# Marking the selected keys on VectorE behind the last pair's mask, a later sum of the gate rows, and an earlier load of the second modulation tile

## The chip, the core and the metric

One core of a Trainium2 chip runs the whole step in one launch. The engines are TensorE (PE in the profile; its weight loads are PEld), VectorE (DVE), ScalarE (ACT), GpSimd (POOL) and SyncE (SP), which issues most transfers. The metric is the device time in microseconds; the runs are compared by their median.

## The reference, cut to what matters

One layer of a decoder: sparse attention with an indexer and retention, side by side, for 1024 new prompt rows and 8 sequences of 4 sample rows (1056 rows in all, D = 1024), all in float32.

```
mod = silu(c) @ w_ada + b_ada;  shift, scale, gate = split(mod, 3)
h   = rms_norm(x, g_norm) * (1 + scale) + shift
qa, ka, va, za, qi, ki, wi, qr, kr, vr, zr, ga, gr = split(h @ w_in)
# sparse attention: score every key with the indexer, keep 256
scores = sum_h relu(qi_h . ki) * wi_h
idx    = top_k(where(admissible, scores, -inf), 256)      # ties: lower index first
y_a    = softmax(qa . ka[idx] / 8) @ va[idx] * silu(za)
# retention: 8 heads, chunks of 128, decay by head; rotary on qr, kr
out    = (q k^T * dmat) v + (q state) * q_decay;  state = decay * state + (k * k_decay)^T v
y_r    = group_norm(out) * g_ret * silu(zr)
merged = sigmoid(ga) * (y_a @ w_pa) + sigmoid(gr) * (y_r @ w_pr)
y      = rms_norm(x + gate * (merged @ w_out), g_final)
```

The keys, values, indexer keys and retention states are outputs too.

## The kernel before, in words

**Products.** PE multiplies float32 matrices as three products of two-part numbers: the high part of the weights with the high part of h, the high part with the low part, and the low part with the high part (L218 to L220, in `terms`). A projection of 128 columns of w_in is 3 chunks of 352 rows, each 8 tiles of the depth times 3 products, so 72 products of 128x352. Each weight tile (512 KB, `ws`) is loaded on SP's queue, rounded by ScalarE (`wh`, L204) and its rest is taken by VectorE or, every third time, by GpSimd (`wl`, L205).

**The head (0 to 62 us).** x is transposed and squared; for each of the 8 depth tiles, `load_wa(k)` loads two tiles of w_ada, `modulation(k)` multiplies them with silu(c) (`ada_rows`, L212) and turns the result, and `h_tile(k)` scales and shifts the tile of h (L340), rounds it (`HH`, ScalarE, L348) and takes the rest (`HL`, VectorE, L349). The first two weight tiles of w_in are loaded behind the first w_ada tile; they are rounded on ScalarE and their rests taken on VectorE (L400). `start_two` (L235) runs the first two projections tile by tile, as the tiles of h arrive.

**The indexer (62 to 140 us)** gives the scores SC[2..7] of the prompt's row blocks (blocks 2 to 7, 384 to 1024 columns wide) and SCS of the sample rows (1056 wide).

**Retention (140 to 545 us)** is four pairs of heads, p = 0 to 3. A pair projects KR, QR, VR, ZR and QA. VR and KR are turned to token rows (PE L543, evicted by ScalarE into `vtok`, L584, and `kd`, L587); z is evicted as `zt` and `zsT` (L595, L596). Then the decayed states (`S`, L611), the products within chunks (PE L621), which VectorE multiplies with the decay mask (L627; the last of the four in a pair is kept as `masked[p]`), and the outputs. The sample rows' small products follow (L663; VectorE's masks `ss`, L666; PE L671). Then the group norm: sums and squares, an rsqrt in 18 columns on VectorE (L162 to L175), the scaling on GpSimd (L695), the transposes back (PE L703), and the last multiplication (`normed[p]`, L706). Behind each pair come a gate's projection, the gate rows (`gate_rows`: products with a part of w_ada, L212 again, a copy by ScalarE L523, a sum over four row groups by PE L525, a second copy L526 and a small transfer L527), and a second gate's projection.

**The selection beside it.** `pick_all` finds for each row of a block the 256th largest score by 31 steps over the bits of the number: VectorE counts for blocks 2 to 6 (L870), ScalarE for block 7 and SCS. The steps stand between the projections of pairs 0 to 3, placed behind entries of `marks`, which hold VectorE's and ScalarE's last instruction at the end of each projection chunk. `exact` repairs thresholds near zero; then `finish(j)` marks the keys of a block: a count above the threshold (L870), the number of ties still to be taken (L918), the row of ties (`eq`, GpSimd, L922), its running sum (L923), two compares (L924, L925), and the multiplication by -1e30 into the mask `bi` (ScalarE, L926). In code order SCS comes first; behind `normed[2]` block 7, then blocks 2 and 3; behind `masked[3]` and one mark each, blocks 4, 5, 6. All blocks share one `eq` and one `ra` tile. The masks of the sample rows are read from 540 us on, those of the blocks in the prompt's attention, from about 820 us.

The rest is the sample attention with its gathers and the projections of K, V and Z (545 to 820 us), the prompt's attention (820 to 960) and the merge.

The order of each engine's instructions is fixed when the kernel is built: a scheduler takes the instructions by their priority in the code and by the `issue_after` marks, and each engine then runs its list in order. What waits holds up everything behind it on that engine.

Of the kernel before, what the change touches and what calls it, by code (L numbers as in the profile page):

```python
# [9 lines left out]
F32R = mybir.dt.float32r  # L10
BF = mybir.dt.bfloat16
I32 = mybir.dt.int32
# [105 lines left out]
def _hybrid_step(ctx, tc, A, outs, dbg):  # L118
# [122 lines left out]
    with ExitStack() as s0:  # L241
# [92 lines left out]
        def h_tile(k, pm):  # L334

            shift = BB[:, k, 0:1]
            nc.scalar.activation(AA[:, k], pm[:, 9:18], AF.Identity, bias=cg[:, k:k + 1], scale=cols[:, 24 + k:25 + k])
            nc.scalar.activation(shift, pm[:, 0:1], AF.Identity, bias=cols[:, k:k + 1])
            h = XT[:, k]
            nc.vector.scalar_tensor_tensor(h[:, :T], h[:, :T], AA[:, k, 0:1], RB[:, :T], op0=OP.mult, op1=OP.mult)  # L340

            nc.vector.tensor_scalar(BB[:, k, 1:9], pm[:, 1:9], cols[:, k:k + 1], shift, op0=OP.add, op1=OP.subtract)
            hs = h[:, T:].rearrange("p (b i) -> p b i", b=NB)
            by_seq = lambda ab: ab[:, k, 1:9].unsqueeze(2).to_broadcast([128, NB, NI])
            nc.vector.tensor_tensor(hs, hs, by_seq(AA), op=OP.mult)
            nc.vector.tensor_tensor(hs, hs, by_seq(BB), op=OP.add)
            for sl in (slice(0, 528), slice(528, TT)):
                high = nc.scalar.activation(HH[k][:, sl], h[:, sl], AF.Identity, bias=shift)  # L348
                rest = nc.vector.scalar_tensor_tensor(HL[k][:, sl], h[:, sl], shift, f32(HH[k][:, sl]), op0=OP.add, op1=OP.subtract)  # L349
            return high, rest  # L350
# [19 lines left out]
        zeros = sp.tile([128, 640], BF, name="zeros")  # L370
        nc.vector.memset(zeros, 0.0)

        def idle_products(n, behind):

            x = pl()
            with tc.issue_after(behind):
                for i in range(n):
                    nc.tensor.matmul(x[:, 512 * (i % 2):512 * (i % 2) + 512], zeros[:, :128], zeros[:, 128:], start=True, stop=True)

        for k in range(KT):  # L380
            load_wa(k)
            if k == 0:
                with tc.issue_after(loads[-1].ins):
                    ws = [wload(wp, w_in, f, 128) for f in (O_KI, O_QI)]
                pm, turned = modulation(k)
                idle_products(8, turned)
            else:
                with tc.issue_after(spread):
                    pm, turned = modulation(k)
            head_ends = h_tile(k, pm)  # L390
            if k == 0:
                for i in (0, 1):
                    wh, wl = [sp.tile([128, KT, 128], F32R, name="w", bufs=4) for _ in "hl"]
                    if i == 0:
                        nc.scalar.copy(wh, ws[i])
                    else:
                        with tc.issue_after(head_ends[0].ins):
                            nc.scalar.copy(wh, ws[i])
                    with tc.issue_after(head_ends[1].ins):
                        nc.vector.tensor_sub(wl, ws[i], f32(wh))  # L400
                    W.append((wh, wl))
# [96 lines left out]
    def retention(gp):  # L498
        with ExitStack() as s3:
# [7 lines left out]
            for p in range(4):  # L507
                rows = split_rows(gp, O_QA + 128 * p, p, q_rows, qs)
                pair(rp, RC, O, SD, p, rows)
                for _ in rows:  # L510
                    pass
                gates(gp, (4 + 2 * p,))
                gate_rows(rp, p)
                gates(gp, (5 + 2 * p,))

    def gate_rows(rp, p):
# [7 lines left out]
        x = pj()  # L524
        nc.tensor.matmul(x[:32, :256], C[:, C_SEL:C_SEL + 32], parts_, start=True, stop=True)  # L525
        nc.scalar.copy(sums[:9], x[:9, :256])  # L526
        nc.scalar.dma_start(GD[:, 256 * p:256 * p + 256], sums[:9])  # L527
# [188 lines left out]

    k_out, v_out, ki_out, st_out, ks_out, vs_out, kis_out, sts_out = outs[2:]

    with ExitStack() as s1:
# [4 lines left out]
        with ExitStack() as s2:  # L724
# [74 lines left out]
            gidx = selp.tile([128, NB], I32, name="gidx")  # L799
            gio = ip.tile([128, NB], I32, name="gio")  # L800
            nc.sync.dma_start(gio, A["gio"])
            with tc.issue_after(whole_row):
                nc.vector.tensor_scalar(ptab, ptab, 16, None, op0=OP.mult)
                nc.vector.tensor_tensor(gidx, ptab, gio, op=OP.add)
            SX = ip.tile([128, 260], F32, name="sx")
# [108 lines left out]
        def finish(j):  # L914
# [7 lines left out]
            nc.gpsimd.tensor_scalar(eq[:n, :W], sc, t, 1.0, op0=OP.is_equal, op1=OP.mult)  # L922
# [3 lines left out]
            nc.scalar.activation(bi, ra[:n, :W], AF.Copy, scale=MASKNEG)  # L926
# [9 lines left out]
        def pick_all():  # L936
# [20 lines left out]
            with tc.issue_after(normed[2].ins):  # L957
                for j in (NP - 2, NV - 1, NV - 2):
                    finish(j)
            for i, j in enumerate(range(NV - 3, -1, -1)):  # L960
                with tc.issue_after(masked[3].ins), tc.issue_after(marks[73 + i][0]):
                    finish(j)
# [75 lines left out]
    QU = 2  # L1038
    NQ = 8 // QU
# [9 lines left out]
    idx = sv.tile([128, NQ, NB], I32, name="idx")  # L1049
    for u in range(NQ):  # L1050
        nc.vector.tensor_scalar(idx[:, u], gidx, float(NQ), float(u), op0=OP.mult, op1=OP.add)
# [452 lines left out]
```

## Time and profile before

| | us |
|---|---|
| median of 3 runs | 1117.72 |
| the runs | 1115.03 to 1120.34 |
| the profiled execution, its own time | 1117.12 |
| its span, first to last instruction | 1115.3 |
| PE busy in it | 1085.7 |
| VectorE busy | 680.3 |
| ScalarE busy | 478.0 |
| GpSimd busy | 253.4 |

The profile is one execution. Its mean granted PE clock was 0.993 of full speed. Rows of the timeline have the start and the length in us, the engine, the line, the operation, the tile written and those read, the shapes, and, in brackets, the idle time of the engine just before and what ended it. "x16" at the end of a PE row is a run of instructions joined to one row. Rows of the windows have, for each stretch, the busy time of each engine, the granted PE clock (1.00 is full), the share of the transfer engines and GB/s. The wait lines have the total, the number of times and the longest in us.

### The profile page before, as it was taken

The numbers are of one execution on the slowest core, as the hardware profiler recorded it, in microseconds if no ns is written. First come the engines' busy times: TensorE is split into PE (matmuls) and PEld (weight loads), VectorE is DVE, ScalarE is ACT, GpSimd is POOL, SyncE is SP. The second block draws the span as 40 slices with busy tenths as digits, with TensorE's granted clock in tenths as the row PEclk, the third lists the DMA queues.
The fourth block names the chain that finished last, engine by engine and source line by source line (L and its number), as shares of the span: only waits on it lengthen the run. The fifth ranks groups of instructions, "written<-read, shape, count | busy, mean of one in ns | idle before, by whom it ended". The sixth has DMA issues, their size and how long they took to land. (4 is left out here: it accounts for less than half of the span.)

```text
span 1115.3 us, 20512 instructions
## 1 busy us (share of the span) xinstructions
PE 1085.7 (97%) x8137; PEld 987.9 (89%) x8138; DVE 680.3 (61%) x1632; ACT 478.0 (43%) x923; POOL 253.4 (23%) x202
## 2 busy tenths in 40 slices
PE   7999999999999999989999999999999999999997
PEld 6889899899989989989999998887988888898776
DVE  6776349698877868888422222210356777497765
ACT  6574445554654455333343333311335666443211
POOL 0003006113311220263242222244113333100000
PEclk9999999999999999999999999999999999999999
DMA  9923335265244515523787757386797520367431
GB/s 308 243 72 105 112 101 151 54 203 140 82 149 126 164 46 181 155 61 92 256 286 232 234 183 247 112 286 240 243 310 273 182 99 30 111 202 257 152 122 58
DMA packets 156024, 185.63 MB, mean 166 GB/s; under 512 B 18630, under 2 KB 126990, under 8 KB 154839
## 3 DMA queue, kind: packets, MB, share of 16 engines
q1 hardware_dynamic: 145632, 147.80, 42.5%
q0 software_dynamic: 9856, 35.66, 9.5%
q8 instruction: 64, 1.05, 0.4%
q10 hardware_dynamic: 438, 0.86, 0.2%
q14 instruction: 34, 0.27, 0.1%
HBM read 139.33 MB, written 41.17 MB: 162 GB/s over the span
## 5 line engine op out<-in xcount | busy, mean ns | idle before, releaser
L218 PE MATMUL pj<-hh,wh 128*128 128x352 f32 (+1 forms) x1168 | 383.4, 328 | 0.3 <-DVE qs L747 0.3
L219 PE MATMUL pj<-hl,wh 128*128 128x352 f32 (+1 forms) x1168 | 379.6, 325 | 0.0
L220 PE MATMUL pj<-hh,wl 128*128 128x352 f32 (+1 forms) x1168 | 378.6, 324 | 0.0
L218 PEld LDWEIGHTS pj<-hh,wh 128*128 128x128 f32 x1168 | 219.8, 188 | 8.2 <-issue 6.7
L219 PEld LDWEIGHTS pj<-hl,wh 128*128 128x128 f32 x1168 | 220.5, 189 | 5.1 <-issue 4.6
L220 PEld LDWEIGHTS pj<-hh,wl 128*128 128x128 f32 x1168 | 219.9, 188 | 4.4 <-issue 4.0
L870 DVE TENSOR_SCALAR_CACHE_REDUCE eq<-sc,cand 128x896 bf16<-128x896 f32 (+4 forms) x155 | 135.7, 876 | 2.6
L204 ACT CAST wh<-ws 128x1024 fp32r<-128x1024 f32 (+1 forms) x65 | 61.0, 942 | 115.4 <-PE pj L219 79.1
L205 POOL TENSOR_TENSOR wl<-ws,wh 128x1024 fp32r<-128x1024 f32 x18 | 45.1, 2506 | 147.0 <-ACT wh L204 146.9
L1223 POOL TENSOR_SCALAR lg<-lg,st 128x1024 f32<-128x1024 f32 (+7 forms) x64 | 48.0, 759 | 122.9 <-DVE st L1222 110.6
L205 DVE TENSOR_TENSOR wl<-ws,wh 128x1024 fp32r<-128x1024 f32 (+1 forms) x47 | 53.3, 1136 | 27.6 <-ACT wh L204 25.6
L1221 ACT ACTIVATE lg<-lg,st 128x1024 f32<-128x1024 f32 (+7 forms) x64 | 49.5, 775 | 25.0 <-DVE st L1220 23.3
L1094 DVE COPY kt<-str 128x512 f32<-128x512 f32 x32 | 22.1, 690 | 55.3 <-PE str L1092 48.0
L1061 POOL DMA_INDIRECT kv<-in_cache_k,idx x32 | 30.1, 941 | 94.2 <-PE str L1092 79.5
L1415 PE MATMUL pj<-woh,MH 128*128 128x512 f32 (+1 forms) x136 | 51.4, 378 | 0.0
L1416 PE MATMUL pj<-wol,MH 128*128 128x512 f32 (+1 forms) x136 | 51.2, 377 | 0.0
L1417 PE MATMUL pj<-woh,ML 128*128 128x512 f32 (+1 forms) x136 | 51.2, 377 | 0.0
L713 ACT ACTIVATE raw<-pj 128x352 f32<-128x352 f32 x48 | 22.1, 462 | 54.1 <-PE pj L220 48.4
L1236 PE MATMUL tr<-C,lg 128*128 128x128 f32 x288 | 43.6, 276 | 1.6 <-POOL lg L1223 0.5
L1061 POOL DMA_INDIRECT kv<-in_cache_v,idx x32 | 30.6, 957 | 52.8 <-PE sx L1122 27.8
L1236 PEld LDWEIGHTS tr<-C,lg 128*128 128x128 f32 x288 | 33.3, 140 | 9.5 <-issue 2.4
L1094 ACT COPY kt<-str 128x512 f32<-128x512 f32 x32 | 18.8, 589 | 50.0 <-PE str L1092 50.0
(352 smaller groups left out, 2002.1 us busy)
## 6 DMA issues: line engine op xcount, KB each, us to landing
ws<-in_w_in SPq DMA_DIRECT2D x51, 512.0 KB
rot<-in_rot SPq DMA_DIRECT2D x8, 1056.0 KB
x<-in_w_ada SPq DMA_DIRECT2D x16, 512.0 KB
TG<-raw SPq DMA_DIRECT2D x15, 528.0 KB
wst<-in_w_out SPq DMA_DIRECT2D x12, 512.0 KB
u<-TG SPq DMA_DIRECT2D x8, 528.0 KB
t<-TG SPq DMA_DIRECT2D x8, 528.0 KB
x<-in_x_prompt SPq DMA_DIRECT2D x8, 512.0 KB
```

What stands on the lines that cost most here:

```text
L204: nc.scalar.copy(wh[:, :, :n], ws[:, :, :n])
L205: (nc.vector if k == 4 or len(order) % 3 else nc.gpsimd).tensor_sub(wl[:, :, :n], ws[:, :, :n], f32(wh[:, :, :n]))
L218: nc.tensor.matmul(p, wh[:, k], HH[k][:, sl], start=(k == 0), stop=False)
L219: nc.tensor.matmul(p, wh[:, k], HL[k][:, sl], start=False, stop=False)
L220: nc.tensor.matmul(p, wl[:, k], HH[k][:, sl], start=False, stop=(k == KT - 1))
L870: nc.vector.tensor_scalar(junk[:n, :W], sc, thr[:n, j:j + 1], 0.0, op0=op, op1=OP.add, accum_out=cnt[:n, j:j + 1])
L1061: nc.gpsimd.indirect_dma_start(out=t.rearrange("p s c -> p (s c)"), out_offset=None, in_=cache.rearrange("g (r s) h d -> (g r) (s h d)", s ...
L1221: nc.scalar.activation(l, l, AF.Exp, bias=st[:, 2:3], scale=0.125, accum_out=st[:, 3:4])
L1236: step["turned"] = nc.tensor.transpose(x[:, 128 * (j - j0):128 * (j - j0) + 128], lg[:, j % 2, 128 * (j // 2):128 * (j // 2) + 128], ident)
L1415: nc.tensor.matmul(x, MH[:, k, tk], wh[:, k], start=(k == 0), stop=False)
L1416: nc.tensor.matmul(x, MH[:, k, tk], wl[:, k], start=False, stop=False)
L1417: nc.tensor.matmul(x, ML[:, k, tk], wh[:, k], start=False, stop=(k == KT - 1))
```

## The change

1. **Marking (`finish`).** The row of ties is made by VectorE (now L934) and no more by GpSimd, and the multiplication by -1e30 by VectorE (L938) and no more by ScalarE. The order: behind `normed[2]` block 7 and block 6; behind `masked[3]`, with no marks, blocks 5, 4, 3 and 2.
2. **Gate rows.** The sum (PE), its copy and its transfer become a function that runs behind the second gate's projection.
3. **Head.** `load_wa` runs one tile ahead, so both loads of w_ada's second tile are issued before the two of w_in. The rounding of the two weight tiles is placed behind the first tile's shift (`moved`) and its last rounding; their rests behind the second tile's scaling (`scaled`) and its last rest. The zeros of the idle products are 512 columns, not 640.
4. `idx` (four tiny VectorE operations that made the gather's indices at 533 us) is made in the indexer's stage.

```diff
@@ h_tile
-            nc.scalar.activation(shift, pm[:, 0:1], AF.Identity, bias=cols[:, k:k + 1])
+            moved = nc.scalar.activation(shift, pm[:, 0:1], AF.Identity, bias=cols[:, k:k + 1])
...
-            nc.vector.scalar_tensor_tensor(h[:, :T], h[:, :T], AA[:, k, 0:1], RB[:, :T], op0=OP.mult, op1=OP.mult)
+            scaled = nc.vector.scalar_tensor_tensor(h[:, :T], h[:, :T], AA[:, k, 0:1], RB[:, :T], op0=OP.mult, op1=OP.mult)
...
-            return high, rest
+            return high, rest, moved, scaled
@@ head
+        rounded, rest = lambda i: nc.scalar.copy(W[i][0], ws[i]), lambda i: nc.vector.tensor_sub(W[i][1], ws[i], f32(W[i][0]))
+        ends = []
+        load_wa(0)
         for k in range(KT):
-            load_wa(k)
+            if k + 1 < KT:
+                load_wa(k + 1)
...
-            head_ends = h_tile(k, pm)
+            ends.append(h_tile(k, pm))
             if k == 0:
                 for i in (0, 1):
...
+                    with tc.issue_after(ends[0][0 if i else 2].ins):
+                        rounded(i)
+            if k == 1:
+                for i in (0, 1):
+                    with tc.issue_after(ends[1][1 if i else 3].ins):
+                        rest(i)
@@ retention
-                gate_rows(rp, p)
+                summed = gate_rows(rp, p)
                 gates(gp, (5 + 2 * p,))
+                summed()
@@ finish
-            nc.gpsimd.tensor_scalar(eq[:n, :W], sc, t, 1.0, op0=OP.is_equal, op1=OP.mult)
+            nc.vector.tensor_scalar(eq[:n, :W], sc, t, None, op0=OP.is_equal)
...
-            nc.scalar.activation(bi, ra[:n, :W], AF.Copy, scale=MASKNEG)
+            nc.vector.tensor_scalar(bi, ra[:n, :W], MASKNEG, None, op0=OP.mult)
@@ pick_all
-            with tc.issue_after(normed[2].ins):
-                for j in (NP - 2, NV - 1, NV - 2):
-                    finish(j)
-            for i, j in enumerate(range(NV - 3, -1, -1)):
-                with tc.issue_after(masked[3].ins), tc.issue_after(marks[73 + i][0]):
-                    finish(j)
+            for behind_, js in ((normed[2], (NP - 2, 0)), (masked[3], range(1, NV))):
+                with tc.issue_after(behind_.ins):
+                    for j in js:
+                        finish(j)
```

What that does to the engines' lists, at three places in the last pair (p = 3). Line numbers grow by 7 in this stretch and by 12 in the marking.

ScalarE, from the last copy of VR's projection (`tmp<-pj`) to vtok's eviction, before; `bi_101` is the mask of block 7, `bi_96` that of block 2:

```order
L559 COPY tmp<-pj_4551 128x352
L926 ACTIVATE bi_101<-ra 128x1024
L595 ACTIVATE zt<-pj 128x352
L596 COPY zsT<-pj 128x352
L584 COPY vtok<-pt 128x512 x2
L926 ACTIVATE bi_96<-ra 128x384
```

and now:

```order
L566 COPY tmp<-pj_4556 128x352
L602 ACTIVATE zt<-pj 128x352
L603 COPY zsT<-pj 128x352
L591 COPY vtok<-pt 128x512 x2
L602 ACTIVATE zt<-pj 128x352
```

The masks stand no more between the evictions.

VectorE, right behind the last product with the decay mask (`masked[3]`), to the second small mask of the sample products (`ss`), before; `sc_783` is block 4's scores, `sc_784` block 5's:

```order
L870 TENSOR_SCALAR eq,cnt<-sc_783,base 128x640
L918 TENSOR_SCALAR rem<-cnt 128x1
L484 TENSOR_TENSOR raw<-pj,raw 128x352
L923 SCALAR_TENSOR_TENSOR ra<-eq 128x640
L924 SCALAR_TENSOR_TENSOR ra<-ra,rem,eq 128x640
L925 SCALAR_TENSOR_TENSOR ra<-sc_783,base,ra 128x640
L870 TENSOR_SCALAR eq,cnt<-sc_784,base 128x768
L666 TENSOR_TENSOR ss<-pb,dm 32x32
L918 TENSOR_SCALAR rem<-cnt 128x1
L666 TENSOR_TENSOR ss<-pb,dm 32x32
```

and now, up to the first of the two small masks:

```order
L882 TENSOR_SCALAR eq,cnt<-sc_784,base 128x768
L930 TENSOR_SCALAR rem<-cnt 128x1
L934 TENSOR_SCALAR eq<-sc_784,base 128x768
L935 SCALAR_TENSOR_TENSOR ra<-eq 128x768
L936 SCALAR_TENSOR_TENSOR ra<-ra,rem,eq 128x768
L487 TENSOR_TENSOR raw<-pj,raw 128x352
L937 SCALAR_TENSOR_TENSOR ra<-sc_784,base,ra 128x768
L882 TENSOR_SCALAR eq,cnt<-sc_783,base 128x640
L938 TENSOR_SCALAR bi_99<-ra 128x768
L930 TENSOR_SCALAR rem<-cnt 128x1
L934 TENSOR_SCALAR eq<-sc_783,base 128x640
L673 TENSOR_TENSOR ss<-pb,dm 32x32
```

Block 5 comes first and stands there whole; block 4's other passes and the count of block 3 (512) stand between the two small masks.

PE, at the transposes of the group norm (L703), before; the gate rows' products (L212) stand 33 projection products ahead of them and the sum (L525) 11:

```order
L220 MATMUL pj<-hh_78,wl 128x352
L218 MATMUL pj<-hh_79,wh 128x352
L219 MATMUL pj<-hl_87,wh 128x352
L220 MATMUL pj<-hh_79,wl 128x352
L703 MATMUL pt<-C,O 128x128 x8
```

and now:

```order
L220 MATMUL pj_5044<-hh_84,wl 128x352
L212 MATMUL pj<-ws,scT 32x128 x13
L710 MATMUL pt<-C,O 128x128 x8
L212 MATMUL pj<-ws,scT 32x128 x3
L218 MATMUL pj<-hh_77,wh 128x352
```

The transposes moved from behind 33 projection products to among the gate rows' products, and the sum (now L531) stands among the second gate's projection, 72 products later.

More of the change, by code (lines that the diff above doesn't have):

```diff
@@ L369, in _hybrid_step @@
         W, ws = [], []
-        zeros = sp.tile([128, 640], BF, name="zeros")
+        zeros = sp.tile([128, 512], BF, name="zeros")
         nc.vector.memset(zeros, 0.0)
@@ L377, in idle_products @@
                 for i in range(n):
-                    nc.tensor.matmul(x[:, 512 * (i % 2):512 * (i % 2) + 512], zeros[:, :128], zeros[:, 128:], start=True, stop=True)
+                    nc.tensor.matmul(x[:, 512 * (i % 2):512 * (i % 2) + 512], zeros[:, :128], zeros, start=True, stop=True)
+        W = [[sp.tile([128, KT, 128], F32R, name="w", bufs=4) for _ in "hl"] for _ in (0, 1)]
+        rounded, rest = lambda i: nc.scalar.copy(W[i][0], ws[i]), lambda i: nc.vector.tensor_sub(W[i][1], ws[i], f32(W[i][0]))
+        ends = []
+        load_wa(0)
         for k in range(KT):
-            load_wa(k)
+            if k + 1 < KT:
+                load_wa(k + 1)
             if k == 0:
@@ L389, in _hybrid_step @@
                     pm, turned = modulation(k)
-            head_ends = h_tile(k, pm)
+            ends.append(h_tile(k, pm))
             if k == 0:
                 for i in (0, 1):
[L393 to L401, printed above, removed]
+                    with tc.issue_after(ends[0][0 if i else 2].ins):
[4 more added lines that the diff above has]
+                        rest(i)
+        head_ends = ends[-1]
         first = start_two(W)
@@ L523, in gate_rows, with summed @@
         nc.scalar.copy(parts_, x[:, :256])
[L524 to L527, printed above, removed]
+        def summed():
+            x = pj()
+            nc.tensor.matmul(x[:32, :256], C[:, C_SEL:C_SEL + 32], parts_, start=True, stop=True)
+            nc.scalar.copy(sums[:9], x[:9, :256])
+            nc.scalar.dma_start(GD[:, 256 * p:256 * p + 256], sums[:9])
+        return summed
     def big(rp, name):
@@ L714, in gates @@
             (nc.scalar if j == 15 else nc.sync).dma_start(TG[128 * j:128 * j + 128], t)
+    QU = 2
+    NQ = 8 // QU
     k_out, v_out, ki_out, st_out, ks_out, vs_out, kis_out, sts_out = outs[2:]
@@ L799, in _hybrid_step @@
             gidx = selp.tile([128, NB], I32, name="gidx")
+            idx = selp.tile([128, NQ, NB], I32, name="idx")
             gio = ip.tile([128, NB], I32, name="gio")
@@ L804, in _hybrid_step @@
                 nc.vector.tensor_tensor(gidx, ptab, gio, op=OP.add)
+                for u in range(NQ):
+                    nc.vector.tensor_scalar(idx[:, u], gidx, float(NQ), float(u), op0=OP.mult, op1=OP.add)
             SX = ip.tile([128, 260], F32, name="sx")
@@ L1036, in rows_in @@
         return hi, lo
-    QU = 2
-    NQ = 8 // QU
     sv = ctx.enter_context(tc.tile_pool(name="sv", bufs=1, reuse_waits="tile"))
@@ L1048, in _hybrid_step @@
     by_pair = lambda d: d[:, T:].rearrange("(h p) c -> p h c", p=128)
-    idx = sv.tile([128, NQ, NB], I32, name="idx")
-    for u in range(NQ):
-        nc.vector.tensor_scalar(idx[:, u], gidx, float(NQ), float(u), op0=OP.mult, op1=OP.add)
     ks, zs, YS = [sv.tile([128, 4, NS], F32, name=n) for n in ("ks", "zs", "ys")]
```

## The prediction

> **What bounds the kernel now.** I read the busy table first, then the waits of TensorE (PE), then PE's own rows around each long wait, and the clock by windows.
>
> ```profile
> PE 1085.7 (97%) x8137; PEld 987.9 (89%) x8138; DVE 680.3 (61%) x1632; ACT 478.0 (43%) x923; POOL 253.4 (23%) x202
> PE pt L212 <- DMA x<-in_w_ada: 2.6, 3, 1.1
> PE pt L543 <- ACT vtok L584: 1.9, 1, 1.9
> PE pb L621 <- DVE tmp L627: 1.3, 2, 1.1
> PE pj L525 <- ACT zt L523: 0.9, 1, 0.9
> ```
>
> PE is busy for 97% of the span of 1115.3 us, so the change, which takes no product out, can only give back idle PE time and time at half clock. The four wait lines (total, times, longest) are the waits that it touches: 2.6 + 1.9 + 1.3 + 0.9 = 6.7 us. The other engines' busy shares say nothing by themselves; what matters is where they hold PE up.
>
> The largest place is the last retention pair (p=3). Rows of the trace there: start, length, engine, line; in brackets the idle time before and who ended it.
>
> ```profile
> 473.77 6.96 POOL L922 TENSOR_SCALAR eq<-sc,base 128x1024 f32<-128x1024 f32 x1 [9.14 <-DVE eq L870]
> 481.38 4.38 POOL L205 TENSOR_TENSOR wl<-ws,wh 128x1024 fp32r<-128x1024 f32 x1
> 480.76 2.83 DVE L923 TENSOR_TENSOR_SCAN ra<-eq 128x1024 f32<-128x1024 f32 x1 [1.53 <-POOL eq L922]
> 483.63 3.22 DVE L924 SCALAR_TENSOR_TENSOR ra<-ra,rem,eq 128x1024 f32<-128x1024 f32 x1
> 486.88 1.28 DVE L925 SCALAR_TENSOR_TENSOR ra<-sc,base,ra 128x1024 f32<-128x1024 f32 x1
> 488.20 1.06 ACT L926 ACTIVATE bi<-ra 128x1024 bf16<-128x1024 f32 x1 [6.80 <-DVE ra L925]
> 489.84 1.09 ACT L584 COPY vtok<-pt 128x512 f32<-128x512 f32 x2
> 490.50 0.28 PE L543 MATMUL pt<-C,tmp 128*32 128x128 f32 x1 [1.90 <-ACT vtok L584]
> 501.32 1.88 DVE L627 TENSOR_TENSOR tmp<-pb,dm 128x512 f32<-128x512 f32 x3
> 502.05 1.09 PE L621 MATMUL pb<-qrT,krT 64*64 64x128 f32 x16 [1.13 <-DVE tmp L627]
> ```
>
> Read it as one story. ScalarE stands 6.80 us in front of the mask of block 7 (L926), which waits for VectorE's L925, which waits for GpSimd's equality row (6.96 us) and a slow L924. Behind that mask, in ScalarE's order, stand the evictions zt, zsT and vtok; PE needs vtok's bank and idles 1.90 us. Later PE waits 1.13 us for VectorE's L627, which stands behind block 3's marking and a weight split. What the clock did then (window; sum, PE busy, PEld, DVE, ACT, POOL, PEclk, DMA share, GB/s):
>
> ```profile
> 488.00:490.00 2.00, 0.60 (x4) 0.31 (x2) 0.87 (x5) 1.80 (x4) 1.13 (x1) 1.00 0.51 152
> 490.00:492.00 2.00, 1.47 (x10) 1.23 (x11) 1.96 (x3) 0.93 (x2) 0.44 (x1) 1.00 0.00 0
> 492.00:494.00 2.00, 2.00 (x9) 2.00 (x8) 1.52 (x5) 1.23 (x4) 0.43 (x1) 0.53 0.00 0
> 494.00:496.00 2.00, 2.00 (x10) 2.00 (x9) 1.01 (x2) 0.61 (x2) 2.00 (x2) 0.62 0.00 0
> 500.00:502.00 2.00, 0.93 (x32) 0.79 (x28) 2.00 (x4) 0.49 (x1) 0.00 (x0) 1.00 0.00 0
> ```
>
> Idle PE: (2.00 - 0.60) + (2.00 - 1.47) = 1.93 us in 488 to 492. Then the granted clock is 0.53 and 0.62 for 4 us, which costs 2.00 x 0.47 + 2.00 x 0.38 = 1.70 us. In 500 to 502 it is 2.00 - 0.93 = 1.07 us, and with the rest of the wait 1.12. Sum of what this pair could give back: 1.93 + 1.70 + 1.12 = 4.75 us.
>
> **Part 1: marking on VectorE, in another order.** The equality row leaves GpSimd and the last multiplication leaves ScalarE; both become VectorE tensor_scalar operations (L934, L938). In ScalarE's order (shown with the change) no mask is left ahead of vtok, so the evictions follow their projections: the 1.93 us and the 1.70 us behind them go. What of the 1.12 us goes, hangs on VectorE, where blocks 2 and 3 (384 and 512 wide) no longer stand ahead of the masked products (L627, now L634), but block 6 does; and four blocks are now held behind the last of those products (`masked`). The order of VectorE shown with the change has them: before, one block of 640 and a count of 768 stood between there and the second small mask of the sample products (L666, now L673); now block 768 whole, block 640 whole and a count of 512. Their prices:
>
> ```profile
> 455.29 0.76 DVE L905 TENSOR_SCALAR eq<-sc,base 128x1024 f32<-128x1024 f32 x1
> 460.69 0.15 DVE L918 TENSOR_SCALAR rem<-cnt 128x1 f32<-128x1 f32 x1
> 466.21 1.26 DVE L575 TENSOR_TENSOR krT<-krT,tmp 128x1056 f32<-128x1056 f32 x1
> 504.24 0.67 DVE L627 TENSOR_TENSOR tmp<-pb,dm 128x512 f32<-128x512 f32 x1
> 511.58 1.01 DVE L870 TENSOR_SCALAR_CACHE_REDUCE eq<-sc,base 128x768 bf16<-128x768 f32 x1
> 515.65 1.76 DVE L923 TENSOR_TENSOR_SCAN ra<-eq 128x768 f32<-128x768 f32 x1 [1.60 <-POOL eq L922]
> 516.06 0.41 PE L671 MATMUL pb<-vtok,ss 32*32 32x64 f32 x4
> ```
>
> The new operations are tensor_scalars of f32; no row of before shows these two, the nearest is L905, 0.76 us for 1024 columns: 0.74 ns a column, and I take it for both. From above they cost what L925 costs (1.28 us, 1.25 ns a column: one operand more). A scan takes 2.3 ns a column (L923), a count and each of L924 and L925 about 1.3, so a whole block 0.74 + 0.74 + 2.3 + 3 x 1.3 = 7.7 ns a column.
>
> I walk VectorE from 460.8, where scs's count is done in before: scs without its count 1056 x 6.4 ns = 6.7 us, blocks 7 and 6 whole 1920 x 7.7 = 14.8, six rotations of 1.26 = 7.5, two splits of 1.23, three products with z of 0.5, and some 2 us behind GpSimd's L205 and its small products: 35.0, so the first masked product starts at about 495.8 and, with ScalarE's third zt on the path, I put it at 496.6. Its three and the scan of the state took from 501.32 to 504.9, 3.6 us: `masked` at 500.2. PE wanted the first at 502.05 - 1.13 = 500.9, now 1.93 + 1.70 earlier, 497.3, when it is there or nearly: the 1.12 us goes too. Behind `masked`: block 768 5.9 us, block 640 5.0, the count of 512 0.7, a split of a row and small rows 0.8, 12.4 in all: the second L673 comes at 512.6. PE wants its product (L671 in before) at 516.06 - 4.75 = 511.3: a **new wait of 1.3 us**. Next is the pair's normalisation:
>
> ```profile
> 532.08 1.35 DVE L691 TENSOR_REDUCE va<-tmp 128x18 f32<-128x1152 f32 x1
> 536.50 2.12 POOL L695 TENSOR_TENSOR O<-O,rs_y 128x1152 f32<-128x1152 f32 x1 [8.59 <-DVE rs_y L694]
> 533.49 1.08 PE L212 MATMUL pj<-ws,scT 128*32 128x128 f32 x32
> 540.61 1.03 PE L703 MATMUL pt<-C,O 128*128 128x128 f32 x8
> ```
>
> In before PE came to these transposes 7.1 us after the gate rows' products (L212) began, with 33 projection products and the sums between; now they stand right behind L212, so PE wants them at 533.49 + 1.0 - 4.75 = 529.7. VectorE has from 512.6: the rest of blocks 640 and 512 and block 384, 6.7 us; the reduction mu, the state's update, the split of a weight and two of rows, 4.9; and what lay between the start of L691 and L695, 4.4 less 0.3 of idx: 15.7, and an estimated 1.3 where it waits for GpSimd's centring and ScalarE's squares: 529.6. Then 2.12 on GpSimd: 531.7. PE is **2.0 us late there in all**, the 1.3 included. Net of this part: 4.75 - 2.0 = 2.75 us. Bounds: 4.75 (no new wait) and, below nothing, what rival D costs. Blocks scs, 7 and 6 lie beside PE's projections and cost nothing as long as the first masked product isn't later than 497.3.
>
> GpSimd loses seven equality rows, and VectorE the time in which both wanted the same port: L205 on GpSimd ends at 481.38 + 4.38 = 485.76, and L924 (1.28 us by itself, like L925) started at 483.63 and ended at 486.85, 1.1 us behind that end. By the Trainium skill, SBUF — State Buffer, section "SBUF: two separate sides", the pair of ports that VectorE and GpSimd share is an exclusive lock for a whole instruction; the trace agrees with that row, and by this rule the new fp32 tensor_scalars would take the lock as well and make GpSimd's splits and vm wait, which nothing here waits for.
>
> **Part 2: the gate rows' sums behind the second gate.**
>
> ```profile
> 333.63 0.62 PE L525 MATMUL pj<-zt,C 128*32 128x256 f32 x2 [0.93 <-ACT zt L523]
> ```
>
> In pair 1 the sum stood right behind the gate rows' products, and PE waited 0.93 us for ScalarE's copy; the other pairs had projection products between (no such wait). Now a whole projection, 72 products, stands between in every pair, so 0.93 us goes. The sums' copy and the small DMA on ScalarE's queue move with it; GD is read after 960 us, so they cost nothing. Bounds: 0 and 0.93.
>
> **Part 3: the head.** Two loads of w_ada (tile 1) go ahead of the two w_in loads; the four still follow each other on SP's queue.
>
> ```profile
> 26.02 0.64 PE L212 MATMUL pt<-x,scT 128*32 128x128 f32 x16 [0.49 <-DMA x<-in_w_ada]
> 27.71 0.64 PE L212 MATMUL pt<-x,scT 128*32 128x128 f32 x16 [1.06 <-DMA x<-in_w_ada]
> 34.71 1.08 PE L212 MATMUL pt<-x,scT 128*32 128x128 f32 x16 [1.08 <-DMA x<-in_w_ada]
> 29.78 1.23 DVE L400 TENSOR_TENSOR w<-ws,w 128x1024 fp32r<-128x1024 f32 x1
> 33.86 1.27 DVE L340 SCALAR_TENSOR_TENSOR xt<-xt,AA,rb 128x1024 f32<-128x1024 f32 x1
> 34.00:36.00 2.00, 1.29 (x17) 0.87 (x18) 2.00 (x4) 0.55 (x2) 0.00 (x0) 0.68 1.17 290
> 36.00:38.00 2.00, 2.00 (x8) 2.00 (x9) 0.21 (x2) 1.49 (x3) 0.00 (x0) 0.50 1.16 297
> ```
>
> A load of 512 KB at 290 GB/s takes 1.8 us, so tile 1's loads land 3.6 us earlier and the waits of 0.49 and 1.06 go; the third wait, 1.08 us for tile 3, stays, since that load has the place it had. Against it, w_in lands 3.6 us later, and the splits of W (L400, now L381, 1.23 us twice) move behind tile 1's scaling, so VectorE's L340 of tile 2 slips from 33.86 to about 35.8. The products in hand cover most of that. I take 1.0 of the 1.55 us; bounds -0.9 (the slip of 1.9 shows in full) and 1.55 (nothing of it shows). The half clock of 34 to 38, 2.00 x 0.32 + 2.00 x 0.50 = 1.64 us, I leave as it is.
>
> The four tiny idx operations, which stood ahead of the rsqrt, are taken off above; the shorter zeros cost nothing.
>
> **Sum**, against the profiled execution's own 1117.12 us: 2.75 + 0.93 + 1.0 = 4.7, so 1112.4 us. The median of the runs is 1117.72, 0.6 above that run, and the runs go from 1115.03 to 1120.34.
>
> **Rivals.** (A) is the forecast, 1112.4. (B) *VectorE takes the whole pair's gain back*: lateness at L673 and L710 of 4.75 us instead of 2.0. For it: my walk has only 0.7 us of slack at `masked`, and 1.3 us of it is an estimate. Against: VectorE no longer waits for GpSimd's equality rows (1.53 and 1.60 in rows above). 1117.12 - 0.93 - 1.0 = 1115.2. (C) *No new wait*, VectorE some 2 us earlier than walked: 1117.12 - 4.75 - 0.93 - 1.0 = 1110.4. (D) *Slower*: the new operations cost 1.25 ns a column, as L925 does. Behind `masked` they are 2 x 2304 columns, 2.35 us more, so PE is 2.0 + 2.35 = 4.35 late; 2176 of the columns lie ahead of L673, 1.1 us, so its wait is 2.4 and that of L710 1.95, each over the 1.93 that half clock followed, at 2 x 1.70. 4.35 + 3.4 - 4.75 = 3.0 lost; with nothing from the head, 1117.12 + 3.0 - 0.93 = 1119.2. It decides where L673's wait reaches 1.93: 0.63 us over 2176 columns, from 1.03 ns a column on. L905's 0.74 speaks against it. (E) *Half clock comes back behind the 1.3 us*: the waits of 0.93 and 1.12 weren't followed by it, the one of 1.93 was. 1112.4 + 1.7 = 1114.1. The Trainium skill, TensorE: Matmul & The Clock Gate, Part 1, has the clock follow a free-running window of 3413 ns, so that the phase decides which gap half clock follows; the trace agrees in length, since 0.94 + 0.76 = 1.70 us lost at half speed is a stretch of 3.4 us. The same page's closing table asks for a gap of some 3 us; the trace's 1.93 differs from that, and the measurement decides.
>
> **How the numbers follow.** Chances: A 0.40, B 0.22, C 0.16, D 0.10, E 0.12. A measurement of this kernel can tell about 0.5% from no change: under 1112.1 is faster, over 1123.3 slower. Faster: somewhat under half of A (0.18), C but for a little (0.14), a bit of B and E (0.02): 0.34. Slower: a fifth of D and what I have not seen: 0.04. The same: 0.62. The range: down to C with the head at 1.55 (1109.8) and some of the runs' spread, 1109.0; up to B with the head at -0.9 (1117.1) and a little spread, 1117.5. Of the cases only D is outside.
>
> **What would show it.** Right: no ScalarE wait of several us ahead of vtok (L591), PE's wait there gone and the clock at 1.00 in 488 to 496; a wait of PE for L673 near 511 and for GpSimd's O (L702) near 530, 2.0 us in all; no wait at L531; waits at the head's L212 once instead of three times; L934 and L938 at 0.74 ns a column. Wrong: those two at over 1 ns, a half-clock stretch behind either new wait, PE late at L634, or the head's first products (L235) waiting for the splits.

## The result and the profile after

| | before | changed |
|---|---|---|
| median, 7 runs each (us) | 1116.36 | 1109.9 |
| the runs (us) | 1115.03 to 1120.34 | 1108.51 to 1110.9 |
| profiled execution, its span (us) | 1115.3 | 1108.1 |
| mean granted PE clock in it | 0.993 | 0.999 |

The ratio is 0.9932, with a 95% interval of 0.9918 to 0.9946: 0.0068 of 1117 us is 7.6 us. The two medians differ by 6.5 us and the two profiled executions by 7.2, all within that interval. The forecast was 1112.4, 4.7 us less than the profiled execution's 1117.12; the time lies inside the range (1109.0 to 1117.5), but outside the half per cent within which the prediction put most of its chance.

The busy table after: PE works 4.2 us less for the same products: before, three stretches ran at half clock (14 to 18, 34 to 39 and 492 to 496 us), now none in which PE has products. GpSimd loses the rows of ties.

```profile
PE 1081.5 (98%) x8138; PEld 982.3 (89%) x8138; DVE 681.4 (61%) x1646; ACT 472.0 (43%) x916; POOL 229.8 (21%) x195
```

PE's waits that answer to the four lines shown of before, and the new ones:

```profile
PE pj L235 <- ACT hh L348: 2.6, 3, 2.0
PE pt L212 <- DMA x<-in_w_ada: 1.9, 2, 1.1
PE pt L710 <- POOL O L702: 0.3, 1, 0.3
PE pb L628 <- DVE tmp L634: 0.2, 1, 0.2
PE pj L218 <- ACT raw L720: 0.8, 1, 0.8
```

The waits for vtok (1.9) and for the sums (0.9) are gone, and that for VectorE's masked products is 0.2 where it was 1.3; the 0.2 that stays is in an earlier pair, at 396 us, and the last pair has none. The wait at the transposes is 0.3 us, where 2.0 were forecast for the small masks and the transposes together. Two waits for ScalarE are new: 2.0 in the head for the rounding of h, and 0.8 for L720, the tanh copies of the gates' projections.

The last pair, rows of VectorE, GpSimd, ScalarE and PE. Everything stands 3.1 us earlier than in before when the pair begins:

```profile
469.72 0.73 DVE L934 TENSOR_SCALAR eq<-sc,base 128x1024 f32<-128x1024 f32 x1
479.21 2.37 POOL L205 TENSOR_TENSOR wl<-ws,wh 128x1024 fp32r<-128x1024 f32 x1
479.64 2.49 DVE L938 TENSOR_SCALAR bi<-ra 128x1024 bf16<-128x1024 f32 x1
480.86 0.47 ACT L602 ACTIVATE zt<-pj 128x352 f32<-128x352 f32 x1 [2.53 <-PE pj L220]
481.55 1.10 ACT L591 COPY vtok<-pt 128x512 f32<-128x512 f32 x2
490.86 1.23 DVE L205 TENSOR_TENSOR wl<-ws,wh 128x1024 fp32r<-128x1024 f32 x1 [0.68 <-ACT wh L204]
492.44 1.88 DVE L634 TENSOR_TENSOR tmp<-pb,dm 128x512 f32<-128x512 f32 x3
495.36 0.66 DVE L634 TENSOR_TENSOR tmp<-pb,dm 128x512 f32<-128x512 f32 x1
507.62 0.17 DVE L673 TENSOR_TENSOR ss<-pb,dm 32x32 f32<-32x32 f32 x1
508.15 0.41 PE L678 MATMUL pb<-vtok,ss 32*32 32x64 f32 x4
524.90 2.12 POOL L702 TENSOR_TENSOR O<-O,rs_y 128x1152 f32<-128x1152 f32 x1 [8.71 <-DVE rs_y L701]
527.08 1.09 PE L710 MATMUL pt<-C,O 128*128 128x128 f32 x8 [0.27 <-POOL O L702]
```

ScalarE waits only for PE's own projections, and vtok is copied at once. VectorE finishes `masked` at 496.0 and the second small mask at 507.8, 0.4 us ahead of PE, which doesn't wait there; GpSimd's scaling ends at 527.0, and the transposes start right behind it: the 0.27 is what is left of the forecast's 2.0. The granted clock over the whole stretch (window; sum, PE, PEld, DVE, ACT, POOL, PEclk, DMA share, GB/s):

```profile
488.00:490.00 2.00, 2.00 (x15) 1.98 (x15) 2.00 (x2) 0.22 (x1) 1.79 (x2) 1.00 0.00 0
490.00:492.00 2.00, 2.00 (x51) 1.79 (x50) 1.32 (x2) 2.00 (x5) 0.00 (x0) 1.00 0.00 0
492.00:494.00 2.00, 2.00 (x44) 1.53 (x40) 2.00 (x5) 0.15 (x2) 0.00 (x0) 1.00 0.32 83
494.00:496.00 2.00, 2.00 (x23) 1.83 (x24) 2.00 (x4) 0.52 (x1) 0.00 (x0) 1.00 0.65 192
```

PE is busy throughout, at full clock. Where the 7.2 us between the two spans came from is read off by the same event in both traces. The first products of the indexer (in rows by line, the two times are the first and last start):

```profile
L782 PEld LDWEIGHTS pl<-kih,qs x40: 186/188/192, 72.4 to 127.9; 128*128 128x128 f32 x40
```

```profile
L791 PEld LDWEIGHTS pl<-kih,qs x40: 186/188/192, 70.2 to 125.6; 128*128 128x128 f32 x40
```

So the head gave 2.2 us (72.4 less 70.2). VectorE's count of scs at the start of the last pair stands at 459.36 before and 456.22 after, 3.1 us apart: pair 1's sum gave the 0.9 between. The rest, 7.2 less 3.1, is 4.1 us, and it comes from the last pair and what follows it. PE's rows divide it: the waits of 1.90 and 1.13 and the 1.70 us by the clock are gone, 4.7 in all; the transposes take 0.27 back. Behind the last sum (L531) PE now waits 0.79 us for the tanh copy of the second gate's third chunk:

```profile
540.50 1.04 ACT L204 CAST wh<-ws 128x1024 fp32r<-128x1024 f32 x1 [3.22 <-PE pj L219]
540.56 0.62 PE L531 MATMUL pj<-zt,C 128*32 128x256 f32 x2
541.45 0.46 ACT L720 ACTIVATE raw<-pj 128x352 f32<-128x352 f32 x1
541.96 0.43 PE L218 MATMUL pj<-hh,wh 128*128 128x352 f32 x1 [0.79 <-ACT raw L720]
```

The kernel keeps two tiles of `pj`. The sum, which stands right behind the second gate's last product, takes one of them, so the next projection needs the one that ScalarE is still to empty, behind a rounding of weights. Last, PE's idle time in the sample attention fell from 2.05 to 1.41 us, which nothing in the change aims at. 4.7 - 0.27 - 0.79 + 0.64 is 4.3, 0.2 more than the 4.1.

### The profile page after: what moved, and what is told of

It is laid out like the page before. It is cut to its first block, busy times and chain, and to the rows that moved or that the text cites. A ratio compares the mean times of both kernels' runs of the same rounds, so it can differ in the third digit from the quotient of the medians.

```text
span 1108.1 us, 20512 instructions
## 1 busy us (share of the span) xinstructions
PE 1081.5 (98%) x8138; PEld 982.3 (89%) x8138; DVE 681.4 (61%) x1646; ACT 472.0 (43%) x916; POOL 229.8 (21%) x195
## 5 line engine op out<-in xcount | busy, mean ns | idle before, releaser
L205 DVE TENSOR_TENSOR wl<-ws,wh 128x1024 fp32r<-128x1024 f32 (+1 forms) x47 | 53.3, 1135 | 35.8 <-ACT wh L204 35.4
L205 POOL TENSOR_TENSOR wl<-ws,wh 128x1024 fp32r<-128x1024 f32 x18 | 43.1, 2395 | 147.9 <-ACT wh L204 147.9
L720 ACT ACTIVATE raw<-pj 128x352 f32<-128x352 f32 x48 | 22.1, 463 | 52.3 <-PE pj L220 46.4
```

The costliest lines, as they stand in the source:

```text
L205: (nc.vector if k == 4 or len(order) % 3 else nc.gpsimd).tensor_sub(wl[:, :, :n], ws[:, :, :n], f32(wh[:, :, :n]))
```

## The experiments

All are timed against the kernel before, and each ratio has its 95% interval. Line numbers are those of each kernel; an edit is against the kernel before unless it says otherwise.

**marking_alone**: part 1 of the change, both engines and order.

```diff
-            nc.gpsimd.tensor_scalar(eq[:n, :W], sc, t, 1.0, op0=OP.is_equal, op1=OP.mult)
+            nc.vector.tensor_scalar(eq[:n, :W], sc, t, None, op0=OP.is_equal)
-            nc.scalar.activation(bi, ra[:n, :W], AF.Copy, scale=MASKNEG)
+            nc.vector.tensor_scalar(bi, ra[:n, :W], MASKNEG, None, op0=OP.mult)
```

with the new loops in `pick_all`.

> The kernel before with part 1 only (marking on VectorE, new order). Theory (the marks on ScalarE and GpSimd held up the last pair's evictions, and half clock followed): PE's wait for vtok (1.9) and for L627 (1.1) and the half clock behind them (1.7) go, less 0.5 of new waits: 4.1 us, a ratio of 0.9963 (0.9950 to 0.9976). Rival (the last pair's gain is worth less by itself, and the rest of the 7 us comes from the head): under 2 us, a ratio over 0.9982.

Measured: 0.9959 (0.9945 to 0.9972), 4.6 us. PE's wait for vtok and that of 1.13 for L627 are gone, 0.6 us at the transposes are new, and no half clock is left in the pair. It carries most of the result. (The four idx operations of part 4 still stand ahead of the rsqrt here and take 0.4 us; whether they make the difference between 0.6 at the transposes and 0.27 in the changed kernel was not tried.)

**mask_alone**: the second pair of lines only.

> The kernel before, with only the last multiplication of the marking moved from ScalarE to VectorE; the row of ties stays on GpSimd and the order of the blocks as before. Theory (ScalarE's list stood behind the mask): the wait for vtok and the half clock behind it go, 3.6 us, ratio 0.9968; the wait for L627 of 1.1 us stays or grows. Rival (GpSimd's slow row and the shared port are the cause, VectorE is late in any case): VectorE's products come as late as before and PE waits for them instead, gain under 1.5 us, ratio over 0.9986.

Measured: 1.0027 (1.0016 to 1.0038), 3 us slower. That is the rival's side and its mechanism, though no loss was expected. ScalarE is free, as meant, and the evictions come at once; but VectorE, behind GpSimd's row of ties, is no earlier, and now makes the masks too:

```profile
PE pb L621 <- DVE tmp L627: 7.1, 2, 7.0
```

```profile
476.33 7.50 POOL L922 TENSOR_SCALAR eq<-sc,base 128x1024 f32<-128x1024 f32 x1 [9.45 <-DVE eq L870]
483.87 2.81 DVE L923 TENSOR_TENSOR_SCAN ra<-eq 128x1024 f32<-128x1024 f32 x1 [1.53 <-POOL eq L922]
495.75 1.97 PE L621 MATMUL pb<-qrT,krT 64*64 64x128 f32 x48
505.56 1.88 DVE L627 TENSOR_TENSOR tmp<-pb,dm 128x512 f32<-128x512 f32 x3
506.30 1.97 PE L621 MATMUL pb<-qrT,krT 64*64 64x128 f32 x16 [6.97 <-DVE tmp L627]
```

The wait of PE has moved from ScalarE's vtok to VectorE's masked product, a few microseconds down, and grown to 6.97 us, with half clock from 504 to 511 us, at its end and behind it. So ScalarE's list was where the lateness showed, not where it arose.

**ties_alone**: the first pair of lines only; the multiplication stays on ScalarE, in the old order.

> The kernel before, with only the row of ties moved from GpSimd to VectorE; the last multiplication stays on ScalarE and the order of the blocks as before. Theory (GpSimd's slow row, and VectorE's chain behind it, bound the last pair; ScalarE's wait was only where it showed): VectorE reaches the end of block 7 ahead of the first zt, ScalarE's mask holds nothing up, ratio 0.9964 (0.9950 to 0.9978), PE's waits for vtok and for L627 together under 1.5 us. Rival (ScalarE's masks in front of the evictions are the cause): the wait for vtok stays, ratio over 0.9985.

Measured: 0.9951 (0.9933 to 0.9969), 5.5 us with one line: the pair's two waits and its half clock are gone. Block 7's tie row takes 0.73 us on VectorE (6.96 on GpSimd in before), its marking ends before zt's projection does, and ScalarE's mask of block 7 stands in nobody's way:

```profile
471.37 0.73 DVE L922 TENSOR_SCALAR eq<-sc,base 128x1024 f32<-128x1024 f32 x1
479.09 1.28 DVE L925 SCALAR_TENSOR_TENSOR ra<-sc,base,ra 128x1024 f32<-128x1024 f32 x1
480.43 1.06 ACT L926 ACTIVATE bi<-ra 128x1024 bf16<-128x1024 f32 x1
483.06 0.47 ACT L595 ACTIVATE zt<-pj 128x352 f32<-128x352 f32 x1 [1.57 <-PE pj L220]
```

On the same chip its median is 1112.76, 1.8 us above that of the next kernel, which moves the mask too (1110.98). Its trace has that difference behind the pair: a wait of 1.83 us for ScalarE's `kx` at 569 us, in the sample attention, which the others don't have. Why it comes there is open.

**engines_old_order**: both pairs of lines, the old order of the blocks.

> The kernel before with both operations on VectorE and the blocks in the old order. Theory (the engines make the gain, not the order): ratio 0.9961 (0.9948 to 0.9975), as marking_alone. Rival (the four blocks behind the last pair's mask make it): ratio at or over 0.998, PE waiting for L627 by 2 us or more.

Measured: 0.9940 (0.9922 to 0.9957), no worse than marking_alone: the engines make the gain. Its profile has no wait for vtok, none of the last pair for L627, and no half clock.

**order_alone**: the new loops in `pick_all` only.

> The kernel before with the new order of the blocks only; ties on GpSimd and the last multiplication on ScalarE. Theory: GpSimd's rows stand in the chain of four blocks between the last mask and the rsqrt, each 1.5 to 3 us more, so PE waits at the small masks or the transposes L703 by 4 us or more, and no gain at vtok: ratio 1.002 to 1.012. Rival (the order by itself frees the evictions): ratio 0.998 or less.

Measured: 1.0039 (1.0019 to 1.0060), slower as expected, but by other waits than named: the wait for vtok stays and one for kd, behind the mask of block 6, is added, with half clock behind each (491 to 496 and 502 to 509 us):

```profile
PE pt L609 <- ACT kd L587: 2.2, 1, 2.2
PE pt L543 <- ACT vtok L584: 1.9, 1, 1.9
```

**doubled_marks**: the changed kernel with L934 and L938 issued twice.

```diff
+            nc.vector.tensor_scalar(eq[:n, :W], sc, t, None, op0=OP.is_equal)
...
+            nc.vector.tensor_scalar(bi, ra[:n, :W], MASKNEG, None, op0=OP.mult)
```

> The changed kernel with both new VectorE operations run twice (same result). They add 0.73 ns a column each: 4.3 us ahead of the last mask, 3.4 behind it. Theory (VectorE is now just in time in the last pair, with some 0.7 us to spare): PE waits for L634 by about 3.5 us and for L702 by some 3 more, half clock follows once or twice: 8 to 12 us slower than the changed kernel, ratio to the kernel before 1.000 to 1.004. Rival (the marks lie beside PE's work with several us to spare): at most 3 us, ratio under 0.996.

Measured: 0.9994 (0.9979 to 1.0008), so 6.9 us (0.0062 of 1117) slower than the changed kernel; between the two expectations, nearer to the first. PE's wait for L634 came, and half clock behind it:

```profile
497.78 1.97 PE L628 MATMUL pb<-qrT,krT 64*64 64x128 f32 x16 [4.34 <-DVE tmp L634]
```

```profile
496.00:498.00 2.00, 0.22 (x2) 0.22 (x4) 2.00 (x4) 0.00 (x0) 0.00 (x0) 0.67 0.06 18
498.00:500.00 2.00, 2.00 (x17) 1.67 (x16) 2.00 (x4) 0.00 (x0) 0.00 (x0) 0.50 0.85 249
500.00:502.00 2.00, 2.00 (x8) 2.00 (x8) 1.97 (x6) 1.90 (x2) 0.00 (x0) 0.50 0.00 0
502.00:504.00 2.00, 2.00 (x10) 2.00 (x9) 1.93 (x3) 0.36 (x1) 0.00 (x0) 0.63 0.09 16
```

The second wait, at the transposes, did not: PE lost 4.3 us idle and, after 498, 2.7 us by the clock (2.00 x 0.50 twice and 2.00 x 0.37), 7.0 in all, more than the 3.4 us that VectorE had to do behind `masked`. VectorE's first masked product starts 41.3 us behind the start of the count of scs (455.70 to 497.04), where it is 36.2 in the changed kernel (456.22 to 492.44). So it came 5.1 us later, 4.3 of them the added work, and PE waited 4.3: VectorE has some 0.8 us to spare at that place in the changed kernel, as the expectation said, although it is busy for only 61% of the span.

**sums_alone**: part 2 of the change.

> The kernel before with the gate rows' sums behind the second gate only. Theory: the wait of 0.93 us in pair 1 goes and nothing else, ratio 0.9992 (0.9980 to 1.0005), PE's wait list without L525 or L531. Rival (the sums' later transfer or copy holds up ScalarE's list elsewhere): a new wait of PE for ScalarE's tanh copies, ratio at or over 1.0.

Measured: 0.9998 (0.9989 to 1.0007). The wait at L525 is gone, but the rival's sign came too: a new wait of PE for a tanh copy, behind the last pair's sum.

```profile
548.55 0.43 PE L218 MATMUL pj<-hh,wh 128*128 128x352 f32 x1 [0.79 <-ACT raw L716]
```

All seven profiled kernels with this part have that wait of 0.79 us; of the seven without it six have no wait for a tanh copy, and order_alone has one of 0.42. The part's net worth in the traces is thus 0.93 - 0.79, some 0.1 us, and the time agrees with that and doesn't tell 0.9 from nothing. In its profile the waits for vtok and for L627's masked products are 1.4 and 2.8 us, where before has 1.9 and 1.3: there more was lost.

**head_alone**: part 3.

> The kernel before with the head's change only. Theory (phase): PE idles no less in the head than before, 6.8 us against 5.5 in 10 to 64 us of the two profiles, and the 2.2 us by which the head ended earlier are 3.4 us of half clock that fell away by the phase of the clock's window: ratio 1.000 (0.9985 to 1.0010), and some profiles of either head show half clock at 14 to 18 or 34 to 38 us, others not. Rival (the earlier load shortens the head by itself): ratio 0.9980 (0.9970 to 0.9988), and no half clock in 30 to 40 us in any profile with the new head.

Measured: 0.9995 (0.9985 to 1.0004), which holds the theory's value and the upper end of the rival's. Here too those waits grew, to 2.1 and 2.9, so what the head gained was in part lost again in the last pair.

**after_again, after_old_order, cast_behind**, three kernels beside each other: the changed kernel; the same with the old loops in `pick_all`; the same with the first rounding of W later:

```diff
-                    with tc.issue_after(ends[0][0 if i else 2].ins):
+                    with tc.issue_after(ends[0][0].ins):
```

> The changed kernel once more, to stand beside the next three on one chip. Every theory: ratio 0.9932 (0.9918 to 0.9946).

> The changed kernel with the blocks in the old order (blocks 7, 2, 3 behind the second pair's normalisation; 4, 5, 6 behind the last mask and one mark each). Theory (the order makes no difference once both operations are on VectorE): the same as the changed kernel within 1 us, ratio 0.9932. Rival (four blocks behind the last mask cost the wait at L702, three cost less or more): over 1 us apart, either way.

> The changed kernel with the rounding of the first weight tile behind the first tile's two roundings of h, not ahead of them. In the changed kernel ScalarE waits 2.15 us for the weight tile's transfer with those two behind it, and PE idles 2.03 us for the first of them. Theory (PE needs the weight tile for its first product in any case, and it lands at 25.4 us): at most 0.3 us of the idle time goes, ratio as the changed kernel. Rival (the two roundings and the rests behind them are what is late): 1 us or more faster, ratio 0.9923 or less.

Measured: 0.9929 (0.9914 to 0.9945), 0.9925 (0.9910 to 0.9941) and 0.9945 (0.9931 to 0.9960). The old order is as fast as the new one, by 0.5 us at the medians (1108.82 and 1109.36) not to be told apart. cast_behind was 1.8 us slower at the median, which neither side expected: its wait for the first product is 1.7 us instead of 2.0, but its scheduler's order of the head changes with the edit, it waits five times for w_ada's loads (3.4 us), and its indexer starts at 72.3.

**head_undone2**: the changed kernel with the old head, its zeros kept at 512 columns. (head_undone, the same with the 640 columns of before, has no time: its tiles need 102.06 KB a partition where 102 are left.)

> The changed kernel with the head as before, but for the zeros' length. The profiles so far put the indexer's first products at 71.7 to 72.4 us with the old head and at 70.2 to 70.3 with the new one, half clock in the head or not. Theory (the head's change is worth its 1.5 to 2 us by itself; the phase is not its cause): ratio to the kernel before 0.9946 (0.9935 to 0.9958), indexer's first products at 71.7 to 72.4. Rival (the difference is phase, the change itself is worth 0.5 us): ratio 0.9935 or less, indexer's first products under 71 us in a profile without half clock.

Measured: 0.9948 (0.9934 to 0.9962), against 0.9932 and 0.9929 for the changed kernel: 1.8 to 2.1 us for the head's change. Each of the ratios is uncertain by 1.6 us, their difference by some 2, so the times alone don't settle it; the traces do, and against the theory that head_alone had been run for, that the head's gain is only the phase of the clock. Two profiles without any half clock in the head show the gain by itself. The window from 10 to 72 us of marking_alone (old head) and of the changed kernel (new head):

```profile
10.00:72.00 62.00, 53.84 (x530) 46.16 (x530) 48.54 (x117) 41.01 (x85) 2.40 (x1) 1.00 0.77 206
```

```profile
10.00:72.00 62.00, 55.23 (x535) 47.05 (x534) 48.29 (x118) 41.63 (x87) 2.41 (x1) 1.00 0.77 214
```

At a clock of 1.00 in both, PE is busy for 1.4 us more of the same 62 us with the new head. The indexer starts at 71.8 and 70.2; over all profiles at 71.5 to 72.4 with the old head (74.5 in mask_alone) and at 69.8 to 70.6 with the new one, with and without half clock (72.3 in cast_behind, whose order of the head is another). Of the 2.2 us between the first two profiles about 1.6 are thus the change's, and 0.6 came with the two stretches of half clock in before.

## Why the prediction was right and where it was wrong

**The pair's idle time: right in size, wrong in its cause.** The three terms that could go (1.93 idle, 1.70 half clock, 1.12 idle) went, 4.75 us in all, and PE's wish for the second small mask, forecast at 511.3, is 508.15 + 3.1 = 511.3. But the story put ScalarE's mask ahead of vtok first and called the evictions freed since no mask was left there. Freeing ScalarE alone did take the wait for vtok away, and still made the kernel slower (1.0027); taking the ties from GpSimd alone took all three terms away (0.9951), with the masks still on ScalarE. The chain was GpSimd's tie row, and VectorE behind it; ScalarE's 6.80 us of idle time was the end of that chain. GpSimd's row is in the prediction's rows, as 6.96 us, but only as one link.

**The new waits: the mis-sized step.** The sum took 2.0 us back for PE being late at the small mask and at the transposes; the changed kernel has 0.27, all of it at the transposes. The walk of VectorE was late by 1.7 us: it put the second small mask at 512.6, and it came at 507.8 + 3.1 = 510.9.

The walk's 35.0 us from the count of scs to the first masked product were right (457.5 to 492.4 in the profile, 34.9), but by luck. The sum adds durations, and each row begins before the last one ends, here by 0.07 us, over the whole stretch by 2.2 us. Against that, GpSimd cost VectorE more than the 2 us of the walk: 1.8 in one L938 (2.49 us, where 1056 columns took 0.69), and 0.7 and 0.9 in an L938 and an L604 beside its product vm; and VectorE stood idle for 0.8 us, most of it for ScalarE's rounding of a weight tile.

```profile
460.76 1.22 DVE L580 TENSOR_TENSOR krT<-krT,rot 128x1056 f32<-128x1056 f32 x1
461.91 1.24 DVE L581 TENSOR_TENSOR tmp<-tmp,rot 128x1056 f32<-128x1056 f32 x1
...
487.55 1.35 DVE L938 TENSOR_SCALAR bi<-ra 128x896 bf16<-128x896 f32 x1
488.82 1.36 DVE L604 SCALAR_TENSOR_TENSOR zsT<-zt,zsT 128x352 f32<-128x352 f32 x1
492.00 0.52 DVE L604 SCALAR_TENSOR_TENSOR zsT<-zt,zsT 128x352 f32<-128x352 f32 x1
...
507.72 0.47 DVE L938 TENSOR_SCALAR bi<-ra 128x640 bf16<-128x640 f32 x1
514.07 2.12 POOL L694 TENSOR_TENSOR O<-O,mu 128x1152 f32<-128x1152 f32 x1 [24.27 <-DVE mu L692]
514.24 2.23 DVE L938 TENSOR_SCALAR bi<-ra 128x512 bf16<-128x512 f32 x1
```

Two things made the walk late. First, 0.8 us were put on top for ScalarE's third zt (495.8 to 496.6); the product with it (L604, at 492.00) starts right behind the row before it. Second, the 12.4 us from `masked` to the second small mask hold block 640 whole, and the stretch behind it counts "the rest of block 640" again: its last multiplication (0.47 us, at 507.72) stands behind the small mask. Without it the walk has 11.9, and 11.8 came (496.0 to 507.8). The stretch behind it fits: 507.8 to 524.8, 17.0 us as walked (15.7 + 1.3): 1.3 were allowed for waits, and one L938 beside GpSimd's centring (L694) took 2.23 us for 512 columns. 2.0 less 1.7 is the 0.3 that was measured.

**The price of the new operations: right.** 0.73 us for the ties of 1024 columns and 0.69 for the mask of 1056, 0.65 to 0.71 ns a column, against the 0.74 taken from L905; the upper bound of 1.25 and with it rival D had no part. Where the new operations met GpSimd, the prediction had GpSimd wait; in these rows VectorE waited, behind a GpSimd row that had begun before it. D's mechanism, a late VectorE with half clock behind, is real all the same: doubled_marks, which adds 0.7 ns a column and operation where that price would have added 0.5, got a wait of 4.3 us and half clock.

**Rival C, no new wait (1110.4), is what came**, 0.5 us from the measured 1109.9; it had a chance of 0.16. Its number is closer than its terms: the head gave more than its 1.0, the sums less than their 0.93, and the sample attention 0.6 that no case has. B (VectorE takes all back) and D did not come. E's question, whether half clock follows a wait, has a mixed answer. In the last pair the waits of 1.87 us and more were followed by half clock (before, order_alone, sums_alone, mask_alone, doubled_marks), those of 1.4 us and less were not; but head_alone's wait of 2.06 us at 488.66 was not followed either, while its next one, 2.71 us, was. The length of the wait alone doesn't decide it.

**The sums: a cost put at nothing.** The 0.93 us are gone from pair 1 (3.1 less 2.2 is 0.9). But "they cost nothing" was reasoned from when the sums are read, not from the tile of `pj` that each sum takes on PE: behind the last pair that brought the new wait of 0.79 us.

**The head: too small, and its waits were others.** The forecast took 1.0; it was some 1.6 by itself, and 2.2 between the two profiles. The wait of 1.08 for tile 3 stayed, as said (1.07), but another of 0.79 is left for a later tile, and the first product waited 2.0 for ScalarE, which stood 2.15 us in front of w_in's transfer with the roundings of h behind it. What paid is for the larger part not at the start: at 56 to 64 us, with the last tile of h, PE idles for 0.81 us with the old head (before and marking_alone) and not at all with the new one, 0.8 of the 1.4 us above. Which of the head's edits does it was not tried. The half clock of 34 to 38, left as it is in the forecast, was absent after; it is not a lasting part of either head.

**The chances.** Measured in the two profiles the terms are 2.2 for the head, 0.93 - 0.79 = 0.1 for the sums, 4.7 - 0.27 = 4.5 for the last pair and 0.6 in the sample attention, against 1.0, 0.93, 2.75 and nothing. With a forecast 0.3 us on one side of the half-per-cent line the prediction said "the same" by 0.62; two terms, each more than a microsecond too small, decided that.

## What to carry to other kernels

When an engine waits long in front of one instruction, follow the chain to the engine that was slow, not the one that holds the queue: freeing ScalarE's queue alone moved PE's wait to VectorE and made it longer, and moving one slow GpSimd operation took the pair's waits away. Walk an engine's list by the rows' starts, and count each row once: durations overlap (2.2 us in 35 here), rows beside GpSimd take longer than alone, and a total can come out right with both wrong; the 1.7 us by which the walk was late were an allowance that no row asked for and a row counted in two stretches. Something moved out of the way takes its buffers with it: the sum that waited no more in pair 1 made the next projection wait in pair 3. An engine that is busy for 61% of the span can have under 1 us to spare at the one place where PE waits for it; doubling the suspected work shows that in one run.

## What the runs showed of the hardware

- One tie row of 1024 columns took 0.73 us on VectorE and 6.96 on GpSimd beside VectorE's rotations; with 640 columns GpSimd took 2.42 us in before, 3.8 ns a column. The Trainium skill, GPSIMD Engine Reference, section "Elementwise — side-by-side cycle accounting", gives about 2.6 cycles an element against VectorE's 1 and a measured ratio of 1.96 for a tensor_tensor. Here, for a tensor_scalar, it is 4.5 for 640 columns (2.42 against VectorE's 0.54 after), and the measurement decides.
- VectorE's L938 of block 7 started at 479.64 and took 2.49 us; GpSimd's L205 beside it ended at 481.58, and 0.55 us later L938 ended. L938 of block 3 (512 columns) took 2.23 us beside GpSimd's centring, and ended 0.3 us behind it, where 640 columns took 0.47 alone. The Trainium skill, SBUF — State Buffer, section "SBUF: two separate sides", has a two-port VectorE operation and a GpSimd one shut each other out for a whole instruction; the trace agrees, and it cost the new operation 1.8 us at each of the two places.
- Half clock in the head came in 5 of 8 profiles of the old head and in 2 of 6 of the new one (cast_behind's counted with it), at 13 to 19, 29 to 34 or 34 to 44 us: the changed kernel had it at 29 to 33 in one profile and not in another. Every stretch in the head took 1.70 us off the clock, as did the one in the last pair of before; behind the waits of 2.2 (order_alone), 4.3 and 7.0 us it was 3.4. The Trainium skill, TensorE: Matmul & The Clock Gate, Part 1, has the window run freely, which fits; that the phase is the cause was not tried.
